# New durations in the cost tables of a list scheduler that orders one Trainium2 kernel's instructions

## The chip, the cores and the metric

The kernel runs on one core of a Trainium2 chip. The metric is the device time of one execution in microseconds; the time before is the median of three runs. PE is the matmul engine, PEld its weight loads, DVE the vector engine, ACT the scalar (activation) engine, POOL the GpSimd engine and SP the engine that issues the DMAs.

## What is computed

256 tokens of 1024 columns go through two stacks of layers, all in float32.

- First stack, four layers: an attention (kinds a, b, c, then a again), a residual and a layer norm, then a feed-forward part (gate, up, silu, down; 2816 hidden columns), a residual and a layer norm.
- Second stack, two layers. Each has one wide projection of the normed tokens, from which four branches are made: a gated convolution, a sparse attention whose keys are the 64 of highest index score per token (found by eight rounds of "take the eight largest, then strike them out"), a gated linear recurrence, and an attention over 256 memory tokens. The branches are lifted to 1024 columns, gated, summed and projected; then comes a feed-forward part as above, with root-mean-square norms in front.

```python
def swiglu(x, w_gate_up, w_down):
    gu = x @ w_gate_up
    gate, up = gu[..., :D_FF], gu[..., D_FF:]
    return (jax.nn.silu(gate) * up) @ w_down
```

## The kernel before, in words

The tokens are two tiles of 128 (`t` = 0 and 1). Every product with weights is done in float32r with both operands split in two parts: `xT` (or `s`) as high and low part of the transposed tokens, `wh` and `wl` as high and low part of the weights; three matmuls of 128x128 by 512 columns per pair of 128 rows (`dense`, L377, its matmul is L390; the down product of the feed-forward part is L1113 to L1115). Weights come in pieces of 256 rows by 512 columns, in one fixed order (`loader`, L349): SP loads a piece into one of 4 `raw` buffers, ACT casts it to `wh` (L366), DVE subtracts to get `wl` (L371), and both tiles use it. There are 8 pairs of `wh`, `wl` buffers.

The smaller matmuls are plain float32: transposes of 128x128 blocks (L440), scores of two heads at a time (L628) and their products with the values (L649), the index scores (L1522), the memory attention (L1738, L1756) and the recurrence (L1949, L1987, L2006 and L2008). For a pair of heads the chain is: scores on PE (L628), mask and row minimum on DVE (L635), exponential with its sum on ACT (L642), reciprocal on DVE (L660), scaling on ACT or DVE (L665 or L668), transpose on PE (L440), copy on ACT or DVE (L451 or L454), product with the values on PE (L649).

**The order of the instructions is a planner's.** All tensors are handled by Python generators, each a chain of work. The class `Flow` (L114) runs them against a clock of its own while the program is written out, and the order in which they issue instructions is the order in every engine's queue. On the chip each engine works through its queue in that order, and semaphores alone hold an instruction back until its inputs are there. So the planner's durations set no time on the chip; they set the order. Each issue is booked:

- `op` (L218) adds a duration to the engine's planned busy time and returns its end plus `LAT`, the time at which the chain goes on.
- `act` (L223), `dve` (L230) and `pool` (L233) turn a number of elements per partition into a duration; `pe` (L236) moves the clock itself on and returns it plus `PELAT`.
- PE is given to the chain of lowest rank among those whose inputs are there by the planner's clock (`rank`, L173): transposes and attention matmuls have ranks 0 to 3, products with weights 5. ACT and DVE are given to the weight casts and subtractions and to some steps of the norms by `grant` (L182); all other steps on them are queued when their chain is resumed.
- `turned` (L447) and `shares` (L651) compare the planned busy times of ACT and DVE to choose which of the two does a copy or a scaling.
- `root` (L1313) is the inverse root of a norm, one POOL instruction (L1315); `rms_heads` (L1343) uses it between a sum and two multiplications on DVE.

```python
def op(self, eng, ns):
    end = max(self.busy[eng], self.cur) + ns
    self.busy[eng] = end
    return end + self.LAT
```

Of the kernel before, what the change touches and what calls it, by code (L numbers as in the profile page):

```python
# [17 lines left out]
S = 256  # L18
D = 1024
NT = S // P  # L20
# [14 lines left out]
SB = 217  # L35
PV = 135
# [33 lines left out]
class Buf:  # L70
    """A buffer out of a Slots, given back with free(when its last reader is through)."""
# [42 lines left out]
class Flow:  # L114
    """Puts the instructions of many chains of work into one order. A chain is a generator. It
    yields a time to go on at, an Event to wait for, a buffer to be given, or ("pe", rank) to
    be given the tensor engine, lowest rank first."""

    LAT = 250.0
# [53 lines left out]
    def rank(self, ask):  # L173
        """The first tile leads in the products with weights, but not by too much."""
        r = ask[0]
        if r == (5, 0) and self.lag > self.limit:
            r = (6, 0)
        elif r[0] == 5 and r[1] >= NT and self.soon:
            r = (4, r[1])
        return r, ask[1]  # L180

    def grant(self, eng):  # L182
        """Lets one of those go on that wait for the engine to be idle: the lowest rank first, and
        those of a rank above 0 not in an urgent stretch, unless they have waited long."""
# [3 lines left out]
        # weights come first when few are at hand  # L188
# [34 lines left out]
    def act(self, n, table=None):  # L223
        ns = n / 1.2 + 120
        if table is not None and table != self.table:
            self.table = table
            ns += 1300
        return self.op("act", ns)

    def dve(self, n):  # L230
        return self.op("dve", n / 0.96 + 75)

    def pool(self, n):  # L233
        return self.op("pool", n * 2.1 + 120)

    def pe(self, ns):  # L236
        # the clock is halved when the last 3.4 us were idle, until as many were busy
# [15 lines left out]
class Parts:  # L253
    """The two parts of a transposed operand, and when each stretch of them is there."""
# [25 lines left out]
class Net:  # L280
    def __init__(self, nc, tc, ctx, t_in, out):
# [22 lines left out]
        # the last token tile never finds all banks taken  # L304
        self.lead = Slots(f, MM - 1, lambda: None)
        # attentions of the second block at a time
# [5 lines left out]
    def pieces(self, tag, n):  # L312
        """Two ways to cut one buffer: for n pairs of heads of up to 768 keys, or 3 n pairs of up to
        256, each head with room for a sink."""
# [26 lines left out]
    def group(self, key, w, *ranges, rows=256):  # L341
        """The pieces of w [k, .], two k tiles each, for column ranges side by side."""
# [6 lines left out]
    def loader(self):  # L349
        nc = self.nc  # L350
        for piece in self.plan:
            shape = [P, piece.srcs[0].shape[1], sum(s.shape[2] for s in piece.srcs)]
            raw = yield self.raw.want(shape)
            at = 0
# [3 lines left out]
            self.f.spawn(self.split(piece, raw, shape, self.f.op("dma", shape[1] * shape[2] * 1.45) + 1800))  # L358
# [18 lines left out]
    def dense(self, t, xt, key, ps):  # L377
        """ps = x^T.T @ the group's pieces, three products per pair of operands, those that need a
        second part when it is there."""
# [5 lines left out]
        count = 0  # L385

        def product(a, b, j, k):
# [3 lines left out]
            f.pe(max(n, 384) / 2.4 + 2.5)  # L391
# [29 lines left out]
    def phase(self, t, name):  # L421
        """How many pieces of weights the first tile may be ahead."""
# [11 lines left out]
    def turn(self, blocks, rank):  # L434
        """The [128, 128] blocks transposed, side by side in a PSUM bank."""
# [8 lines left out]
    def turned(self, blocks, dst, rank):  # L444
        """dst [128, n, 128] = the blocks transposed."""
# [13 lines left out]
    def parts(self, h, l, blocks, rank, hev=None, lev=None):  # L459
        """h, l [128, n, 128] = the two parts of the blocks transposed."""  # L460
# [19 lines left out]
    def pair(self, n):  # L480
        """Room for the parts, with n events."""
# [4 lines left out]
    def parts_x(self, x, rank, hurried=False, late=0.0, then=None):  # L486
        """The two parts of the transpose of x [128, 1024]; the second half of x is there at the
        time late."""
# [33 lines left out]
    def setup(self):  # L522
        """What the first layer needs besides weights."""
# [13 lines left out]
        # angles, for [positions, token tile, frequency]  # L537
# [8 lines left out]
        # whole turns, split into a multiple of 4096 and a rest, are taken off in three steps  # L546
# [14 lines left out]
        # both into [-pi, pi]  # L561
# [10 lines left out]
        # per positions and token tile [128, 2, 2, 8]: cos | cos, and -sin | sin  # L572
# [12 lines left out]
    def rotate(self, q, nh, tab):  # L585
        """The first 16 of each of nh heads of q [128, nh, 64], in place; the time it is done."""
# [15 lines left out]
    def heads(self, t, two, l, m, left):  # L602
        """Two heads of one token tile, whose q^T and k^T lie in different halves of the rows. Each:
        its q^T per group; per PSUM bank a list of (group, k^T blocks [64, 128]) and the mask over
        them; the V blocks [128 keys, 64] in the same order; where its output's transpose goes,
        [64, 128]; what its -maximum starts from; minus its sink, if any. Their sums l and -maxima
        m; the count of pairs left and the event for the last."""
# [12 lines left out]
        for j in range(len(two[0][1])):  # L620
# [8 lines left out]
            yield f.pe(2 * SB * len(both[0][0]))  # L629
            for z, (head, (ks, mask), ps, s) in enumerate(zip(two, both, pss, scs)):  # L630
# [6 lines left out]
                ends[z] = f.dve(wb + 40)  # L637
                ps.free(ends[z])
            at += wb
        for z, s in enumerate(scs):  # L640
            yield ends[z]
            nc.scalar.activation(s[:, :w], s[:, :w], AF.Exp, scale=-1.0, bias=m[:, z:z + 1], accum_out=l[:, z:z + 1])  # L642
            end = f.act(n + 220, "exp")
# [7 lines left out]
        f.pe(2 * PV * nb)  # L651
# [1424 lines left out]
```

## Time and profile before

| | us |
|---|---|
| median of three runs | 2458.12 |
| lowest and highest of the three | 2455.24 and 2460.45 |
| span of the profiled execution, first to last instruction | 2453.7 |
| PE busy in it | 2416.1 (98%) |
| DVE, ACT, POOL busy in it | 1601.5 (65%), 1209.8 (49%), 116.0 (5%) |

The profiled execution's own time is not listed apart from its span; the runs lie 1.5 to 6.8 us above the span. A busy time is the union of an engine's instructions. Matmuls are pipelined and their ends are modelled, so the time that one matmul adds to a row of them is read from their starts, not from its duration. The granted clock (PEclk) is 1.00 when TensorE runs at the upper of its two levels (2.4 GHz) throughout a stretch, and 0.50 at the lower one.

### The profile page before, as it was taken

The page shows a single profiled execution, that of the slowest core. Times are in us where ns is not written, and L with a number is a line of the kernel's source. Part 1 is how long each engine was busy: PE and PEld are TensorE (multiplying, and loading weights), DVE is VectorE, ACT ScalarE, POOL GpSimd, SP SyncE. Part 2 cuts the span into 40 slices and gives each one's busy share as a digit, 9 for nine tenths or more (in the row PEclk, how much of TensorE's full clock was granted, in tenths as well). Part 3 has the DMA queues.
Part 4 walks back from the last instruction along what each step waited for, and adds up shares of the span by engine and source line. Part 5 has one row for each costly group of instructions (what it writes and reads, how often), then busy time and mean ns, then how long its engine had stood idle before and what let it go on. Part 6 is the DMA issues. An engine that isn't in the chain of part 4 may idle for free.

```text
span 2453.7 us, 32501 instructions
## 1 busy us (share of the span) xinstructions
PE 2416.1 (98%) x12163; PEld 1953.6 (80%) x12163; DVE 1601.5 (65%) x2600; ACT 1209.8 (49%) x1779; POOL 116.0 (5%) x151
## 2 busy tenths in 40 slices
PE   8999999999999999999999999999999999999999
PEld 6688888888888778887788778878888778878887
DVE  7754666567546675467854887676754786776544
ACT  5544445455444654446544456444544465445443
POOL 0000000000000000010000100111000100111000
PEclk9999999999999999999999999999999999999999
DMA  7365563544656446554665536655765445655654
GB/s 240 114 208 170 175 220 115 162 129 155 196 167 195 152 149 206 168 184 134 206 199 172 180 112 182 179 155 178 235 187 168 142 139 160 181 152 190 192 172 129
DMA packets 226238, 419.84 MB, mean 171 GB/s; under 512 B 18048, under 2 KB 66848, under 8 KB 226080
## 3 DMA queue, kind: packets, MB, share of 16 engines
q1 hardware_dynamic: 226080, 417.76, 55.2%
q8 instruction: 95, 1.56, 0.3%
q14 instruction: 63, 0.52, 0.1%
HBM read 416.66 MB, written 1.05 MB: 170 GB/s over the span
## 4 chain that ended last, share of the span: by engine, by line
PE 94%; DVE 3%; ACT 1%; DMA 1%; issue 0%; POOL 0%; SPq 0%; DVEq 0%; ACTq 0%; POOLq 0%
PE mm L390 68%; PE acc L440 5%; PE acc L1113 5%; PE acc L1115 5%; PE acc L1114 5%; PE acc L628 2%; PE acc L649 2%; DVE wl L371 1%; ACT wh L366 0%; DVE s L1537 0%; DVE s L1557 0%; DMA raw<-w_in 0%; PE acc L1738 0%; PE acc L1756 0%; PE acc L2008 0%
## 5 line engine op out<-in xcount | busy, mean ns | idle before, releaser
L390 PE MATMUL mm<-wh,xT 128*128 128x512 f32 x5056 | 1642.5, 396 | 11.1 <-ACT wh L366 3.6
L371 DVE TENSOR_TENSOR wl<-raw,wh 128x1024 fp32r<-128x1024 f32 (+1 forms) x764 | 933.9, 1231 | 584.0 <-ACT wh L366 582.0
L366 ACT CAST wh<-raw 128x1024 fp32r<-128x1024 f32 (+1 forms) x764 | 795.8, 1046 | 804.8 <-PE mm L390 570.7
L390 PEld LDWEIGHTS mm<-wh,xT 128*128 128x128 f32 x5056 | 945.5, 188 | 218.1 <-issue 5.9
L390 PE MATMUL mm<-wl,xT 128*128 128x512 f32 x2528 | 973.2, 390 | 3.3 <-DVE wl L371 3.1
L390 PEld LDWEIGHTS mm<-wl,xT 128*128 128x128 f32 x2528 | 475.8, 189 | 95.7 <-DVE wl L371 5.2
L1113 PE MATMUL acc<-wh,s 128*128 128x512 f32 x528 | 211.7, 401 | 0.0
L1115 PE MATMUL acc<-wh,s 128*128 128x512 f32 x528 | 208.2, 394 | 0.0
L1114 PE MATMUL acc<-wl,s 128*128 128x512 f32 x528 | 208.1, 394 | 0.0
L1115 PEld LDWEIGHTS acc<-wh,s 128*128 128x128 f32 x528 | 99.2, 188 | 23.4
L1114 PEld LDWEIGHTS acc<-wl,s 128*128 128x128 f32 x528 | 99.4, 188 | 21.3
L1113 PEld LDWEIGHTS acc<-wh,s 128*128 128x128 f32 x528 | 99.3, 188 | 20.9
L440 PE MATMUL acc<-ident,s 128*128 128x128 f32 x624 | 94.7, 273 | 4.5 <-DVE s L1358 4.5
L440 PEld LDWEIGHTS acc<-ident,s 128*128 128x128 f32 x624 | 77.0, 140 | 26.0 <-DVE s L1358 5.2
L1315 POOL TENSOR_TENSOR brs<-brs,mhalf 128x1 f32<-128x1 f32 x28 | 24.9, 890 | 1464.4 <-DVE brs L942 1216.8
L464 ACT CAST xT<-acc 128x512 fp32r<-128x512 f32 x68 | 39.8, 586 | 93.0 <-PE acc L440 92.9
L642 ACT ACTIVATE sc<-sc,m 128x129 f32<-128x129 f32 (+5 forms) x128 | 67.1, 526 | 23.7 <-DVE m L635 23.6
L464 ACT CAST s<-acc 128x512 fp32r<-128x512 f32 (+1 forms) x72 | 39.6, 550 | 65.9 <-PE acc L440 65.7
L454 DVE COPY pT<-acc 128x512 f32<-128x512 f32 (+1 forms) x84 | 48.7, 597 | 35.2 <-PE acc L440 34.8
L469 DVE TENSOR_TENSOR xT<-acc,xT 128x512 fp32r<-128x512 f32 x68 | 46.7, 687 | 34.9 <-ACT xT L464 34.7
L1071 ACT ACTIVATE s<-mm 128x512 f32<-128x512 f32 (+1 forms) x72 | 40.3, 560 | 53.1 <-PE mm L390 52.7
L440 PE MATMUL acc<-ident,sc 128*128 128x128 f32 x368 | 58.3, 283 | 6.3 <-ACT sc L665 6.1
(187 smaller groups left out, 1447.8 us busy)
## 6 DMA issues: line engine op xcount, KB each, us to landing
raw<-w_gate_up SPq DMA_DIRECT2D x160, 512.0 KB, 4.0
raw<-w_in SPq DMA_DIRECT2D x144, 512.0 KB, 4.2
raw<-w_down SPq DMA_DIRECT2D x88, 512.0 KB, 3.3
raw<-ffn_w_up SPq DMA_DIRECT2D x80, 512.0 KB, 3.7
raw<-b_w_qkv SPq DMA_DIRECT2D x96, 256.0 KB, 3.1
raw<-ffn_w_down SPq DMA_DIRECT2D x44, 512.0 KB, 3.3
raw<-w_lift SPq DMA_DIRECT2D x32, 512.0 KB, 4.0
raw<-a_w_qkv SPq DMA_DIRECT2D x24, 512.0 KB, 5.2
```

The costliest lines, as they stand in the source:

```text
L366: nc.scalar.copy(h[:], raw[:])
L371: nc.vector.tensor_sub(l[:], raw[:], h[:])
L390: nc.tensor.matmul(ps, a[:, k, :], b[:, k % 2, :], start=count == 1, stop=count == 3 * (last + 1))
L440: nc.tensor.transpose(ps[:, j * P:(j + 1) * P], b, self.ident[:])
L454: self.nc.vector.tensor_copy(dst, p3)
L464: self.nc.scalar.copy(h, p3)
L628: nc.tensor.matmul(ps[:, b * P:(b + 1) * P], head[0][g], k, start=True, stop=True)
L642: nc.scalar.activation(s[:, :w], s[:, :w], AF.Exp, scale=-1.0, bias=m[:, z:z + 1], accum_out=l[:, z:z + 1])
L649: nc.tensor.matmul(head[3], head[2][b], pT[:, (z * nb + b) * P:(z * nb + b + 1) * P], start=b == 0, stop=b == nb - 1)
L1113: nc.tensor.matmul(a, hh[:, k, :], wh[:, 0, cs], start=ch == 0 and k == 0, stop=False)
L1114: nc.tensor.matmul(a, hh[:, k, :], wl[:, 0, cs], start=False, stop=False)
L1115: nc.tensor.matmul(a, hl[:, k, :], wh[:, 0, cs], start=False, stop=ch == 5 and k == nk - 1)
```

## The change

Only what the planner books is changed; every instruction's form stays as it is. The constants and formulas of `act`, `dve`, `pool`, `pe`, `loader`, `root` and `LAT` get other values, `act` and `dve` get a further argument for accumulator reads and per-partition scalars, and every group of small float32 matmuls is booked at `FP` = 112 ns a matmul plus `SWITCH` = 190 ns instead of `SB` = 217 ns a matmul. Comments and docstrings become empty lines, and two lines are added at the top, so line numbers after are higher by 2.

```diff
-SB = 217
-PV = 135
+FP = 112.0
+SWITCH = 190.0
+POINTER = 170.0
+SUM = 190.0
...
-    LAT = 250.0
+    LAT = 60.0
...
-    def act(self, n, table=None):
-        ns = n / 1.2 + 120
+    def act(self, n, table=None, more=0.0):
+        ns = 0.904 * n + 127 + more
...
-    def dve(self, n):
-        return self.op("dve", n / 0.96 + 75)
+    def dve(self, n, more=0.0):
+        return self.op("dve", n / 0.96 + 152 + more)
...
-        return self.op("pool", n * 2.1 + 120)
+        return self.op("pool", n * 2.3 + 130)
...
-            self.f.spawn(self.split(piece, raw, shape, self.f.op("dma", shape[1] * shape[2] * 1.45) + 1800))
+            self.f.spawn(self.split(piece, raw, shape, self.f.op("dma", shape[1] * shape[2] * 1.53) + 2000))
...
-            f.pe(max(n, 384) / 2.4 + 2.5)
+            f.pe(max(n / 2.4 * 1.0625, FP))
...
-            yield f.pe(2 * SB * len(both[0][0]))
+            yield f.pe(2 * FP * len(both[0][0]) + SWITCH)
...
-                ends[z] = f.dve(wb + 40)
+                ends[z] = f.dve(wb, 142.0)
...
-            end = f.act(n + 220, "exp")
+            end = f.act(n, "exp", POINTER + SUM)
...
-        f.pe(2 * PV * nb)
+        f.pe(2.2 * FP * nb + SWITCH)
...
-                ends.append(f.act(n))
+                ends.append(f.act(n, None, POINTER))
...
-                    end = f.pe(648)
+                    end = f.pe(690)
...
-        return self.f.pool(60 + n)
+        return self.f.op("pool", 1050.0)
...
-            end = f.pe(2 * SB * (t + 1))
+            end = f.pe(2 * FP * (t + 1) + SWITCH)
...
-        yield f.pe(2 * SB * NT)
+        yield f.pe(4 * FP * NT + SWITCH)
...
-        end = f.pe(4 * SB)
+        end = f.pe(8 * FP + SWITCH)
...
-        end = f.pe(1950)
+        end = f.pe(16 * FP + SWITCH)
```

## Rows read from the trace of the kernel before

**Rows 1.** The page: the span, and each engine's busy time, share and instructions.

```profile
span 2453.7 us, 32501 instructions
...
PE 2416.1 (98%) x12163; PEld 1953.6 (80%) x12163; DVE 1601.5 (65%) x2600; ACT 1209.8 (49%) x1779; POOL 116.0 (5%) x151
```

**Rows 2.** Busy time by stretch: length, busy per engine, granted clock, DMA share, GB/s.

```profile
0.00:45.00 45.00, 37.30 (x173) 30.30 (x174) 31.87 (x74) 21.97 (x25) 2.73 (x22) 1.00 0.73 245
45.00:85.00 40.00, 33.21 (x227) 21.78 (x226) 33.92 (x115) 27.88 (x82) 3.19 (x16) 0.91 0.50 161
85.00:1120.00 1035.00, 1030.14 (x5308) 835.69 (x5307) 644.08 (x1015) 505.48 (x707) 17.08 (x24) 1.00 0.55 170
1120.00:1175.00 55.00, 51.30 (x346) 36.46 (x346) 43.37 (x125) 38.04 (x113) 4.39 (x21) 0.94 0.30 96
...
1380.00:1455.00 75.00, 71.34 (x402) 55.63 (x402) 66.82 (x194) 41.48 (x88) 10.29 (x8) 1.00 0.46 141
...
1900.00:1975.00 75.00, 68.13 (x359) 54.71 (x358) 59.54 (x153) 34.63 (x64) 6.90 (x6) 0.98 0.46 135
1975.00:2454.00 479.00, 474.94 (x2290) 386.81 (x2288) 302.58 (x411) 228.70 (x314) 32.38 (x23) 1.00 0.55 166
```

**Rows 3.** The chain that ended last: start, length, what.

```profile
2055.38 61.94 PE mm L390 x273
```

**Rows 4.** Timeline, 1960 to 1971 us: start, length, engine, line [idle before, releaser].

```profile
1964.91 0.28 DVE L1535 MAX8 m<-s 128x8 f32<-128x128 f32 x1
...
1965.50 0.42 DVE L1535 MAX8 m<-s 128x8 f32<-128x256 f32 x1
...
1966.36 0.28 DVE L1535 MAX8 m<-s 128x8 f32<-128x128 f32 x1
...
1969.53 0.50 PE L390 MATMUL mm<-wl,xT 128*128 128x512 f32 x1 [2.56 <-DVE wl L371]
```

**Rows 5.** Timeline, 1908 to 1923 us.

```profile
1915.77 1.10 ACT L464 CAST xT<-acc 128x512 fp32r<-128x512 f32 x2
...
1917.00 1.92 POOL L1315 TENSOR_TENSOR ss<-ss,mhalf 128x4 f32<-128x4 f32 x1 [2.92 <-DVE ss L1352]
...
1918.96 0.69 DVE L1355 TENSOR_TENSOR s<-mm,ss 128x512 f32<-128x512 f32 x1 [0.31 <-POOL ss L1315]
...
1920.43 0.80 PE L440 MATMUL acc<-ident,s 128*128 128x128 f32 x4 [4.19 <-DVE s L1358]
```

**Rows 6.** Groups by line and shape: count | busy us, mean ns | idle before.

```profile
L366 ACT CAST wh<-raw 128x1024 fp32r<-128x1024 f32 x756 | 791.7, 1052 | 791.1 <-PE mm L390 560.9 <-PE acc L1115 128.2 <-DMA raw<-w_in 14.3
...
L371 DVE TENSOR_TENSOR wl<-raw,wh 128x1024 fp32r<-128x1024 f32 x756 | 929.4, 1238 | 578.8 <-ACT wh L366 576.9
...
L1315 POOL TENSOR_TENSOR ss<-ss,mhalf 128x4 f32<-128x4 f32 x12 | 14.6, 1221 | 63.7 <-DVE ss L1352 63.7
```

**Rows 7.** Timeline, 45 to 85 us (first attention).

```profile
51.28 0.62 PE L440 MATMUL acc<-ident,sc 128*128 128x128 f32 x2 [1.78 <-ACT sc L665]
...
53.66 2.92 ACT L366 CAST wh<-raw 128x1024 fp32r<-128x1024 f32 x3
...
55.12 3.48 DVE L371 TENSOR_TENSOR wl<-raw,wh 128x1024 fp32r<-128x1024 f32 x3
...
66.16 0.50 ACT L642 ACTIVATE sc<-sc,m 128x257 f32<-128x257 f32 x1
...
66.66 0.50 ACT L642 ACTIVATE sc<-sc,m 128x257 f32<-128x257 f32 x1
```

**Rows 8.** Timeline, 1126 to 1140 us (last attention of kind a).

```profile
1130.01 0.40 PE L390 MATMUL mm<-wl,xT 128*128 128x512 f32 x1
...
1130.34 0.49 PE L628 MATMUL acc<-s,s 64*128 64x128 f32 x4
...
1130.76 0.50 PE L390 MATMUL mm<-wh,xT 128*128 128x512 f32 x1
...
1131.10 0.40 PE L390 MATMUL mm<-wl,xT 128*128 128x512 f32 x1
```

More of the change, by code (lines that the diff above doesn't have):

```diff
@@ L929, in square @@
         self.nc.scalar.activation(out, src, AF.Square, scale=1.0 / 32, bias=bias, accum_out=acc)
-        return self.f.act(out.shape[-1] + 220)
+        return self.f.act(out.shape[-1], None, POINTER + SUM)
     def norm(self, t, r, old, gb, st):
@@ L1747, in recall_two @@
                                  accum_out=l[:, z:z + 1])
-            end = f.act(S + 220, "exp")
+            end = f.act(S, "exp", POINTER + SUM)
         ps.free(end)
@@ L1757, in recall_two @@
                                  pT[:, (NT * z + b) * P:(NT * z + b + 1) * P], start=b == 0, stop=b == NT - 1)
-        pT.free(f.pe(2 * SB * NT))
+        pT.free(f.pe(4 * FP * NT + SWITCH))
         self.through(left)
@@ L1987, in hgrn @@
                 nc.tensor.matmul(ps[:, h * P:(h + 1) * P], ken[rr, h, :], v[rr, h, :], start=True, stop=True)
-            yield f.pe(4 * SB)
+            yield f.pe(8 * FP + SWITCH)
             s2 = yield self.s.want([P, 4, P])
```

## The prediction

> **What bounds the kernel now.** I read the page first: PE is busy for 2416.1 of 2453.7 us [rows 1], so 37.6 us of idle PE is all that an order alone can win, apart from how fast PE's own work runs. The second view is the busy time by stretch [rows 2]; the reader is to subtract PE's busy time from each length. The start loses 7.70 us (0 to 45) and the last stretch 4.06 us; the one waits for first loads, the other holds the way out, and I count neither. What is left lies in five stretches: 6.79 us (45 to 85, first attention), 4.86 (85 to 1120), 3.70 (1120 to 1175, the other attention of kind a), 3.66 (1380 to 1455, first layer of the second stack) and 6.87 (1900 to 1975, its second layer), 25.9 us in all. In three of them the granted clock is 0.91, 0.94 and 0.98: stretches at the lower of the two levels (1.2 GHz, against 2.4) that follow idle PE. At 0.09 x 40, 0.06 x 55 and 0.02 x 75 they cost at most 8.4 us more. So at most some 34 us, 1.4%, can be won. The third view, the chain that ended last, gives PE's pace: 273 products in 61.94 us, 0.2269 us each [rows 3]. The planner booked 215.8 ns, 5% too fast, and books 226.7 after.
>
> The last views are timelines of the waits, to see whether a wait comes from a wrong booking, which the change can mend, or from a lack of other work, which it can't.
>
> **The change part by part.** The same instructions are issued (the counts of matmuls, casts and DMAs stay), so nothing is added or removed on any engine. Every term is a wait that moves, and the sum is made against the span of 2453.7 us; the median of the runs, 2458.1, is 4.4 us longer, and I carry the difference over.
>
> *The eight rounds of the index selection.* A round is two DVE operations of n columns each. On the chip a round of 128 columns goes from 1964.91 to 1965.50 (0.59 us) and one of 256 from 1965.50 to 1966.36 (0.86) [rows 4]. Before, they were booked at 2 x (n / 0.96 + 75), that is 0.42 and 0.68 us; after, at 2 x (n / 0.96 + 152), 0.57 and 0.84. Both tiles' rounds run in turn, so eight of each were booked 8 x (0.17 + 0.18) = 2.8 us short. Behind them in DVE's queue stands a subtraction that makes wl, and PE waits 2.56 us for it at 1969.53 [rows 4]. The new booking is short by 8 x 0.04 = 0.3 us only, so that subtraction goes ahead of some of the rounds, or other products ahead of its own. I take 2.3 us as won; cover for the rounds pushed back is there, since the sparse branch is the third to be lifted.
>
> *The same code in the first layer of the second stack*: PE idle 3.66 us while DVE is busy for 66.8 of 75 [rows 2]. I take half, 1.8 us; the bounds are 0 and 3.66.
>
> *The root of a norm.* POOL takes 1221 ns on average for four heads [rows 6], and 1.92 us at 1917.00, where PE then waits 4.19 us for transposes that hang on it [rows 5]. From the root's start to the transposes pass 3.43 us; the old booking was 254 + 250 for the root and 2 x 608 + 250 for the two multiplications, 1.97 us; the new one is 1110 + 2 x 685 + 60, 2.54 us. The casts of another operand end at 1916.87 [rows 5], so products with weights could run, but they stand behind the transposes. Transposes booked 0.57 us later let two or three products of 0.227 past: 0.6 us won. The low clock after this wait stays, as most of the wait does.
>
> *LAT from 250 to 60, and longer operations.* POOL ends at 1918.92 and DVE starts at 1918.96 [rows 5]: a hand-off is 0.04 us, so 60 covers it. A DVE operation of 512 columns on the path was booked at 608 + 250 = 858 ns and takes 0.69 + 0.04; it is now booked at 745. Plans were late by 0.13 us a step and are now late by 0.01: still on the safe side, so I see no new waits from it. In the attentions the steps of a pair hardly change: exponential plus sum of 256 columns 767 before, 778 after; scaling 583 and 588. So the 10.5 us idle there (6.79 and 3.70) are mostly no error of booking: PE waits for ACT, 1.78 us at 51.28 [rows 7], when the projections are through and little else is there. Bounds 0 and 10.5; I take 2 us, nearer to none, for the copies that come 0.11 to 0.15 us earlier.
>
> *85 to 1120 us*: 4.86 us in 1035; I take 0, with the same to either side as bounds.
>
> *Weights, DMAs, POOL's and SP's queues.* A piece is booked at 1053 + 1219 ns for ACT and DVE (973 + 1142 before; rows say 1052 and 1238 [rows 6]); against 12 products of 0.227, 2.7 us, either fits. DMAs are booked 0.28 us later a piece; SP's queue holds them in the same fixed order of pieces, and a load waits for a free buffer, not for the booking: 0. POOL is busy for 5% [rows 1]: 0. Copies and scalings that change from ACT to DVE or back by the planned busy times cost PE nothing where both are under 65%: 0.
>
> Sum: 2.3 + 1.8 + 0.6 + 2.0 = 6.7 us, from 2453.7 to 2447.0 of span, or 2458.1 to **2451** us.
>
> **The rivals.** *Slower: pairs are booked too far apart.* The durations of a row are not what an engine needs per instruction when it runs several. Three casts in a row take 2.92 us with the last at 1.05, so 0.94 apart, and three subtractions 3.48, so 1.12 apart [rows 7]; booked are now 1.05 and 1.22. Exponentials of 257 columns start 0.50 us apart (66.16, 66.66) [rows 7]; booked were 0.52, and are now 0.72. With the scalings a pair of heads of 256 keys now takes 2 x 718 + 2 x 528 = 2.5 us of ACT's plan instead of 1.7. So its later pairs become ready in the plan one by one, and where two groups of small matmuls stood side by side, products with weights come between. The Trainium skill (Perfetto Trace Analysis, Optimizing Scalar/DVE Operations) says that a profiled duration holds a write acknowledgement which overlaps the next instruction; the rows agree (1.238 us long, 1.12 apart), and by that rule the change books both engines too full.
>
> What an extra alternation costs: from the product at 1130.01 over two small matmuls (four records) to the second product after them, 1131.10, pass 1.09 us; less two products at 0.227 this is 0.64 [rows 8]. Of it 0.10 is the way in (0.33 instead of 0.227) and 0.11 the way out, and the matmuls themselves stay. So an alternation costs between 0.21 and 0.64 us; I take the middle, 0.43. The code has 214 groups of small matmuls other than transposes (112 of scores, 88 with values, 14 of the recurrence). If one in eight loses its neighbour, 27 x 0.43 = 11.6 us, and the waits that I count as won come back elsewhere: 2458.1 + 11.6 = **2470** us. It decides from some 16 more alternations (6.7 / 0.43) on. For it speaks that the plan's shift is large on ACT; against it, that a mask and a copy on DVE lie between the pairs anyway, and that shorter hand-offs work the other way.
>
> *No change.* The waits come from a lack of other work: both tiles go through the same steps close behind one another, and when one wait is mended the next dependency shows. The change then does not do what it says where it matters: the order around a wait stays as it is. The 1.78 us at 51.28, and the 4.19 of which the new booking covers 0.57, speak for it. **2458** us.
>
> *Faster by more.* Better bookings let products with weights fill half of the 25.9 us and of the 8.4 at the low clock: 17 us, **2441** us. For it speaks that products with inputs ready did stand behind a wait (1916.87 against 1920.43); against it, that only the rounds and the root were booked far off.
>
> **How the numbers follow.** About 0.2% (5 us) is what a measurement of this kernel can tell from no change: its three runs lie 5.2 us apart. Any new order of 32501 instructions shuffles waits by some us, so I leave the chances wide: the forecast 0.36 (its own range 2446 to 2455), more 0.14, no change 0.22, slower 0.28. Faster by over 0.2% (under 2453.2) holds the case of more and nearly all of the forecast's, 0.48; within 0.2% the case of no change and the forecast's rest, 0.24; slower 0.28. The range reaches from the larger gain, 2441, to the price of the slower rival, 2470; beyond lie one in ten on either side.
>
> **What would show it.** Right: at the end of the selection in both layers of the second stack PE waits for wl under 0.5 us; the stretch 1900 to 1975 has 3 us less idle PE; products with weights stand between the root of the memory keys and their transposes; matmul counts are the same. The slower rival: PE's busy time rises above 2416 us by several us, with idle time the same or less, and more changes between L628 or L649 and L390. No change: the five stretches keep their idle time, or trade it. Wrong altogether would be a new wait of several us for wh or wl after an attention, or a low clock in more places.

## The result: slower by 0.76%, and the profile after

| | before | after |
|---|---|---|
| median of four runs, us | 2457.46 (2455.24 to 2460.45) | 2474.26 (2471.89 to 2477.24) |
| ratio, 95% interval | | 1.0076 (1.0063 to 1.0090) |
| span of the profiled execution | 2453.7 | 2472.9 |
| PE idle in it | 37.6 | 48.6 |

The changed kernel is 17 us slower by the medians, 19 by the ratio; 2451 us was foretold, with 2470 as the upper end. In the code after, every line number is higher by 2. The page of the kernel after, span and engines:

```profile
span 2472.9 us, 32489 instructions
...
PE 2424.3 (98%) x12163; PEld 1959.2 (79%) x12163; DVE 1596.8 (65%) x2596; ACT 1212.7 (49%) x1783; POOL 117.3 (5%) x151
```

Against [rows 1], PE has the same 12163 matmuls, 8.2 us more busy time and 11.0 us more idle time; that is the 19.2 us of span. The products themselves did not get slower, as one row of the chain that ended last shows (start, length, what): 16.34 us for 72, 0.2269 us each, as in [rows 3].

```profile
171.26 16.34 PE mm L392 x72
```

So the busy time grew elsewhere. Busy time by stretch of the kernel after, columns as in [rows 2]:

```profile
45.00:90.00 45.00, 36.72 (x242) 26.02 (x241) 32.74 (x114) 28.09 (x91) 6.44 (x16) 0.85 0.37 119
90.00:570.00 480.00, 479.05 (x2616) 390.78 (x2614) 300.61 (x489) 235.22 (x319) 5.41 (x4) 1.00 0.51 164
570.00:625.00 55.00, 51.10 (x281) 41.74 (x281) 40.11 (x62) 28.15 (x37) 2.05 (x2) 0.97 0.48 158
...
1130.00:1190.00 60.00, 54.75 (x354) 39.58 (x353) 45.73 (x119) 38.22 (x104) 3.17 (x16) 0.91 0.30 97
...
1390.00:1485.00 95.00, 90.41 (x506) 71.68 (x506) 81.92 (x224) 52.61 (x117) 10.64 (x10) 0.98 0.42 133
1485.00:1915.00 430.00, 429.06 (x2043) 350.29 (x2042) 278.19 (x344) 208.26 (x258) 29.99 (x24) 1.00 0.57 184
1915.00:1990.00 75.00, 67.90 (x332) 54.47 (x331) 53.20 (x128) 34.25 (x59) 7.46 (x7) 0.95 0.49 150
```

And one stretch of the kernel before, which [rows 2] holds only as part of a longer one:

```profile
560.00:615.00 55.00, 53.87 (x334) 44.17 (x335) 43.66 (x69) 30.94 (x41) 1.47 (x2) 1.00 0.55 171
```

Idle is length less busy; the price of the clock is at most (1 - granted clock) x length, since PE is idle in some of that time anyway. The stretches after start up to 15 us later and are up to 20 us longer, to hold the same work; both columns in us:

| stretch | idle before, after | clock before, after |
|---|---|---|
| first attention | 6.79, 8.28 | 3.6, 6.8 |
| end of the attention of kind b | 1.13, 3.90 | 0, 1.7 |
| last attention of kind a | 3.70, 5.25 | 3.3, 5.4 |
| first layer of the second stack | 3.66, 4.59 | 0, 1.9 |
| second layer of the second stack | 6.87, 7.10 | 1.5, 3.8 |
| sum | 22.2, 29.1 | 8.4, 19.5 |

These five short stretches hold 7 of the 11.0 us more idle and up to 11 us more of the lower clock, most of the loss; between them (90 to 570, 1485 to 1915) PE is busy for 99.8% of the time at full clock. I also counted the products of dense groups along both traces and compared the start of the same count: after is late by 3.7 us at 110, 2.8 at 520, 7.4 at 604, 12.5 at 1192, 13.9 at 1497, 15.5 at 1890 and 20.1 at 1940 us (times of before). The loss comes in steps, at those places, and stays nearly flat between them.

Part of the first step is a wait for loads. The setup of the second stack transposes two small constants in the first attention; in the kernel after, PE reaches them 4 to 5 us after their loads were issued and waits 2.04 us; before, it came to them 7.6 us after and did not wait. The rest of that stretch's idle time is 6.24 us, no more than the 6.79 before. After:

```profile
63.59 0.20 PE L1265 MATMUL acc<-ident,lbrows 8*128 8x8 f32 x1 [1.03 <-DMA lbrows<-hgrn_lower_bounds]
...
64.79 0.45 PE L1267 MATMUL acc<-ident,cwr 12*128 12x12 f32 x2 [1.01 <-DMA cwr<-conv_w]
```

Before:

```profile
70.75 0.22 PE L1263 MATMUL acc<-ident,lbrows 8*128 8x8 f32 x1
```

**A wait that the prediction did not see.** The stretch at the end of the attention of kind b has the cleanest step, 4.6 us: 2.7 us come with one wait and the lower clock behind it, most of the rest with two waits of 0.85 and 0.73 us (606.88 and 608.70) in the feed-forward part that follows. The first wait is the one to explain. The timeline of the kernel after (start, length, engine, line [idle before, releaser]):

```profile
573.72 0.92 ACT L644 ACTIVATE sc<-sc,m 128x768 f32<-128x768 f32 x1
574.54 0.18 ACT L644 ACTIVATION_READ_ACCUMULATOR sc<-sc,m 128x1 f32 x1
574.61 1.22 DVE L373 TENSOR_TENSOR wl<-raw,wh 128x1024 fp32r<-128x1024 f32 x1
574.64 0.92 ACT L644 ACTIVATE sc<-sc,m 128x768 f32<-128x768 f32 x1
...
577.00 0.39 PE L392 MATMUL mm<-wh,xT 128*128 128x512 f32 x1
577.43 0.69 DVE L985 SCALAR_TENSOR_TENSOR x<-x,mm 128x512 f32<-128x512 f32 x1 [1.60 <-PE mm L392]
...
578.76 0.15 DVE L662 RECIPROCAL l<-l 128x2 f32<-128x2 f32 x1
578.95 1.97 ACT L667 ACTIVATE sc<-sc,l 128x768 f32<-128x768 f32 x2 [2.38 <-DVE l L662]
...
579.71 4.43 PE L442 MATMUL acc<-ident,sc 128*128 128x128 f32 x24 [2.32 <-DVE bmv L942]
...
606.88 0.66 PE L442 MATMUL acc<-ident,s 128*128 128x128 f32 x4 [0.85 <-DVE s L1085]
...
608.70 0.50 PE L392 MATMUL mm<-wh,xT 128*128 128x512 f32 x1 [0.73 <-ACT xT L466]
```

The second row closes the exponentials of the first pair of heads at 574.72, so its reciprocal (L662) could have run at 575.83, after the subtraction. But in DVE's queue it stands behind the residual of the other tile (L985), and DVE sits idle for 1.60 us until the last product with weights has ended (577.39). So the reciprocal starts 2.9 us late, the scaling (L667) with it, and PE, which has just done its last product, waits until it can transpose the scaled scores. The row says bmv, a DVE operation at 579.48; what the transposes read is the scaling. The same place before:

```profile
572.71 0.16 DVE L660 RECIPROCAL l<-l 128x2 f32<-128x2 f32 x1
...
574.23 0.93 ACT L665 ACTIVATE sc<-sc,l 128x768 f32<-128x768 f32 x1
574.52 1.57 PE L440 MATMUL acc<-ident,sc 128*128 128x128 f32 x12
574.72 0.69 DVE L983 SCALAR_TENSOR_TENSOR x<-x,mm 128x512 f32<-128x512 f32 x1
...
576.05 0.15 DVE L660 RECIPROCAL l<-l 128x2 f32<-128x2 f32 x1
...
577.22 1.71 PE L440 MATMUL acc<-ident,sc 128*128 128x128 f32 x12 [1.13 <-ACT sc L665]
```

There the first pair's reciprocal stands ahead of the residual (L983), and its twelve transposes follow the products without a gap; only the second pair's transposes wait, 1.13 us.

The bookings allow the swap. The exponentials stand 0.92 us apart on the chip. Before, each was booked (768 + 220) / 1.2 + 120 = 943 ns, near that. After, it is 0.904 x 768 + 127 + 360 = 1181 ns, even more than the 1.00 us from the start of one to the end of its read (573.72 to 574.72), and the read overlaps the next exponential. So the two exponentials of a pair are booked 0.48 us longer than before, the four 0.95; the hand-off behind them is booked 0.19 us shorter, so a pair's reciprocal is planned some 0.29 us later. A residual can then be ready first in the plan, while on the chip the exponentials are early and the residual is late. That this alone made the swap is argued, not shown; the runs below that change one part bear on it.

### The profile page after: what moved, and what is told of

It is laid out like the page before. It is cut to its first block, busy times and chain, and to the rows that moved or that the text cites. A ratio compares the mean times of both kernels' runs of the same rounds, so it can differ in the third digit from the quotient of the medians.

```text
span 2472.9 us, 32489 instructions
## 1 busy us (share of the span) xinstructions
PE 2424.3 (98%) x12163; PEld 1959.2 (79%) x12163; DVE 1596.8 (65%) x2596; ACT 1212.7 (49%) x1783; POOL 117.3 (5%) x151
## 4 chain that ended last, share of the span: by engine, by line
PE 94%; DVE 3%; ACT 1%; DMA 1%; issue 1%; POOL 0%; SPq 0%; DVEq 0%; ACTq 0%; POOLq 0%
PE mm L392 68%; PE acc L442 5%; PE acc L1115 5%; PE acc L1117 5%; PE acc L1116 5%; PE acc L651 2%; PE acc L630 2%; DVE wl L373 1%; ACT wh L368 0%; DMA raw<-w_in 0%; PE acc L1524 0%; PE acc L2010 0%; PE acc L1989 0%; PE acc L1758 0%; DMA raw<-a_w_qkv 0%
## 5 line engine op out<-in xcount | busy, mean ns | idle before, releaser
L442 PEld LDWEIGHTS acc<-ident,s 128*128 128x128 f32 x624 | 76.4, 141 | 29.1 <-DVE s L1360 5.0
L456 DVE COPY pT<-acc 128x512 f32<-128x512 f32 (+1 forms) x77 | 45.1, 597 | 38.5 <-PE acc L442 38.0
L1073 ACT ACTIVATE s<-mm 128x512 f32<-128x512 f32 (+1 forms) x72 | 40.3, 560 | 50.0 <-PE mm L392 49.5
```

Of the source, the lines that this page charges most:

```text
L442: nc.tensor.transpose(ps[:, j * P:(j + 1) * P], b, self.ident[:])
```

## The experiments

Theories at the start. **A**: a duration is not what an engine needs per instruction; ACT and DVE are booked too full. **B**: 60 ns of hand-off leaves a plan without slack. **C**: any new order costs, since the old one is a chosen one; later in a sharper form, the planner's other settings fit the old bookings. **D**: groups of small matmuls are booked too short. **E**: with products booked at their true pace, the plan puts too few under each step. F and G, below, are rivals of the sharper C. No experiment changes which operations are done, only their order and which of ACT and DVE does a copy or a scaling. In two of the orders, e5_dense and e8_occ, the kernel's result is off by 4.9% all the same, so some step there depends on the order by more than the plan says; which one is not known. Both are timed with the same matmuls as the others, but carry less weight. The table has all medians, the ratio to before with its interval, and PE's idle time in the profiled execution (its span less PE busy). Where the text says what a run costs, it is the ratio less one, times 2456 us:

| run | median us | ratio (95%) | PE idle us |
|---|---|---|---|
| e1_lat | 2458.64 | 1.0017 (1.0007 to 1.0026) | 38.2 |
| e2_pe | 2476.53 | 1.0090 (1.0073 to 1.0106) | 50.1 |
| e3_dur | 2481.86 | 1.0112 (1.0096 to 1.0128) | 49.5 |
| e4_lat245 | 2455.76 | 1.0001 (0.9991 to 1.0011) | 38.7 |
| e5_dense | 2462.03 | 1.0025 (1.0013 to 1.0037) | 40.5 |
| e6_small | 2465.70 | 1.0037 (1.0026 to 1.0048) | 40.5 |
| e7_lat_occ | 2469.27 | 1.0057 (1.0040 to 1.0074) | 41.3 |
| e8_occ | 2471.99 | 1.0060 (1.0035 to 1.0085) | 46.7 |
| e9_dense_mid | 2464.89 | 1.0040 (1.0028 to 1.0052) | 38.5 |
| e10_lat300 | 2460.92 | 1.0016 (1.0005 to 1.0028) | 39.9 |
| e11_pelat260 | 2458.50 | 1.0012 (1.0001 to 1.0023) | 38.9 |
| e12_after_bc5 | 2475.33 | 1.0078 (1.0048 to 1.0107) | 50.5 |
| e13_tuned | 2467.80 | 1.0043 (1.0030 to 1.0057) | 43.4 |
| e14_pitch | 2470.44 | 1.0060 (1.0043 to 1.0078) | 44.0 |
| e15_pitch_tuned | 2455.39 | 1.0000 (0.9991 to 1.0009) | 43.0 |
| e16_cross | 2463.14 | 1.0030 (1.0018 to 1.0041) | 40.7 |
| e17_equal1 | 2464.34 | 1.0043 (1.0028 to 1.0058) | 49.3 |
| e18_equal2 | 2458.67 | 1.0021 (1.0010 to 1.0031) | 38.3 |

### The change in three parts, each alone in the kernel before

e1_lat, the hand-off alone:

```diff
-    LAT = 250.0
+    LAT = 60.0
```

> The kernel before with LAT at 60 instead of 250 and nothing else of the change. Theory A (engines overbooked: the durations of ACT and DVE are latencies, and plan a pair's steps too far apart) expects no loss from this part: 2453 to 2461 us. Theory B (a hand-off without slack: a chain is resumed so early that PE's queue holds instructions whose inputs are just not there) expects most of the loss here: 2469 to 2477 us, with PE idle for 45 us or more. Theory C (the order before is a lucky one among many near-equal orders, and any shuffling costs about the same) expects 2463 to 2475 us here and in every other part alone.

e2_pe, all bookings of PE (the lines with `SB`, `PV`, 648 and 1950, and `dense`):

```diff
-            f.pe(max(n, 384) / 2.4 + 2.5)
+            f.pe(max(n / 2.4 * 1.0625, FP))
...
-            yield f.pe(2 * SB * len(both[0][0]))
+            yield f.pe(2 * FP * len(both[0][0]) + SWITCH)
```

> The kernel before with only PE's bookings of the change (products at 226.7 ns, groups of small matmuls at 112 ns a matmul plus 190). Theory A and theory B expect no loss: 2453 to 2461 us, or a small gain, since the booking of a product now agrees with its pace in the trace. Theory C expects 2463 to 2475 us.

e3_dur, the bookings of ACT, DVE, POOL, DMA and the root, with LAT still 250:

```diff
-        ns = n / 1.2 + 120
+        ns = 0.904 * n + 127 + more
...
-        return self.op("dve", n / 0.96 + 75)
+        return self.op("dve", n / 0.96 + 152 + more)
```

> The kernel before with only the bookings of ACT, DVE, POOL and the DMAs of the change, LAT at 250. Theory A expects the whole loss here or more, 2470 to 2482 us, since chains are booked even later than in the change, with LAT on top. Theory B expects none, 2453 to 2461 us. Theory C expects 2463 to 2475 us.

The hand-off costs 4 us, PE's bookings 22, the durations 28: B falls as the main cause. The parts do not add up: together they cost 19 us, less than either of the two large ones.

### Controls: does any other order cost?

e4_lat245 and e10_lat300 change LAT by little, e11_pelat260 the end of PE's work:

```diff
-    LAT = 250.0
+    LAT = 245.0
```

> A control: the kernel before with LAT at 245 instead of 250, a change of 2% in one booking that means nothing by itself, but gives another order. Theories A and B expect the time of before, 2453 to 2461 us. Theory C expects an order about as bad as any other: 2463 to 2475 us, or in any case a move of 5 us or more.

```diff
-    LAT = 250.0
+    LAT = 300.0
```

> A control without any claim to truth: the kernel before with LAT at 300 instead of 250, all else as before. Hand-offs are booked still later than they are, so no theory of a truer or a tighter plan says anything of it. Theory C expects a loss of 4 to 20 us, 2460 to 2476 us, at the same places as in the other runs; if it takes the time of before, 2452 to 2459 us, then the losses so far belong to the bookings that were changed and not to any new order.

```diff
-PELAT = 200.0
+PELAT = 260.0
```

> A second control of the kind: the kernel before with PELAT at 260 instead of 200, so that results of PE are booked 60 ns later. Theory C expects 2460 to 2476 us; if the losses belong to the changed bookings, 2452 to 2459 us.

They cost 0, 4 and 3 us. A reshuffle as such costs little, so C in its first form gives a fifth of the loss at most; but none of the three is faster than before.

### PE's bookings in halves

```diff
-            f.pe(max(n, 384) / 2.4 + 2.5)
+            f.pe(max(n / 2.4 * 1.0625, FP))
...
-                    end = f.pe(648)
+                    end = f.pe(690)
```

> The kernel before with one part of PE's bookings alone: products with weights at 226.7 ns (and 690 for three down products), their pace in the trace, instead of 215.8 (648). The second run lost 22 us with all of PE's bookings. Theory D (the groups of small matmuls are now booked too short, so the plan crowds the attention steps) expects no loss here: 2450 to 2460 us. Theory E (with the products' true pace the plan has 5% fewer of them under every step of ACT and DVE, whose bookings stay as they were) expects most of the 22 us here: 2468 to 2478 us. Theory C (any shuffling of this size costs) expects 2463 us or more here and in the next run too.

e6_small takes the other lines of e2_pe: `FP` and `SWITCH` in place of `SB`, `PV` and 1950.

```diff
-            yield f.pe(2 * SB * len(both[0][0]))
+            yield f.pe(2 * FP * len(both[0][0]) + SWITCH)
...
-        f.pe(2 * PV * nb)
+        f.pe(2.2 * FP * nb + SWITCH)
```

> The kernel before with the other part of PE's bookings alone: groups of small matmuls at 112 ns a matmul plus 190 a group instead of 217 a matmul. Theory D expects most of the 22 us here, 2468 to 2478 us; theory E expects none, 2450 to 2460 us; theory C 2463 us or more.

```diff
-            f.pe(max(n, 384) / 2.4 + 2.5)
+            f.pe(max(n, 384) / 2.4 + 8.0)
...
-                    end = f.pe(648)
+                    end = f.pe(664)
```

> The kernel before with products booked at 221.3 ns (and 664 for three down products), half-way to the true pace; the whole way cost 6 us. Theory E (the loss grows with the pace booked) expects about half of it, 2457 to 2461 us. Theory C (each new order draws its own waits at the few places where both tiles run out of products) expects no relation: it may be worse than the whole way or as good as before, anywhere from 2453 to 2475 us.

Products cost 6 us, small groups 9, both together 22. Half of the correction of the products costs 10, not half of 6 (the two intervals overlap): no grading, so E falls as a law, and D explains its 9 us only.

Most of these 9 us are lost at the end of the attention of kind b, and by another order than in the changed kernel: by the count of products e6_small is 2.4 us late at 545 and 9.2 at 604. The first pair's reciprocal stands ahead of the residual there (577.07 against 577.39 us), but the second pair's (581.77) stands behind two steps of the norm that start at 580.45, and PE waits 3.00 us. In e2_pe the same wait is 3.37 us:

```profile
584.92 1.97 PE L440 MATMUL acc<-ident,sc 128*128 128x128 f32 x8 [3.37 <-ACT sc L665]
```

### Occupancy instead of duration

e7_lat_occ is e1_lat and e3_dur together, e8_occ the changed kernel, both with this:

```diff
-        self.busy[eng] = end
+        self.busy[eng] = end - {"act": 100.0, "dve": 80.0}.get(eng, 0.0)
```

> The kernel before with LAT at 60 and the new bookings of ACT, DVE, POOL and the DMAs, but an engine is held for 100 ns (ACT) or 80 ns (DVE) less than an instruction's booked duration, as the starts in a row show (three casts 0.94 us apart, three subtractions 1.12); the chain still goes on at the booked end. PE's bookings as before. Theory A (overbooked engines) expects this to lose nothing, 2450 to 2460 us, since the third run lost 27 us with the bookings too full. Theory C expects 2463 us or more.

> The changed kernel with the same correction: ACT and DVE held for 100 and 80 ns less than the booked duration. All of the planner's numbers then agree with the trace to a few per cent. If the change was slow because its numbers were still wrong (theory A, with the loss of PE's part a loss of being out of step with the others), this gives 2450 to 2460 us. Theory C, in which a truer plan is no better than another, expects 2463 to 2480 us.

Both stay at 1.006: A is not the whole cause. How much the correction won in e7_lat_occ is not known, since the two parts without it were not run together. e7_lat_occ also tells what the swap needs. It has it, with PE's bookings as before, while in e1_lat and in e3_dur the first pair's reciprocal stands ahead of the residual (570.26 against 572.92 us, 584.86 against 586.56). So neither the hand-off nor the durations alone gave the swap, and PE's bookings were not needed for it:

```profile
576.58 0.69 DVE L985 SCALAR_TENSOR_TENSOR x<-x,mm 128x512 f32<-128x512 f32 x1 [1.38 <-PE mm L392]
...
577.91 0.15 DVE L662 RECIPROCAL l<-l 128x2 f32<-128x2 f32 x1
```

In e8_occ the step at the end of the attention of kind b is gone by the count of products (1.2 us late at 520, 0.9 at 604), though the reciprocal still stands behind the residual there; PE's wait is 1.18 us instead of 2.32, because more products were left. The correction was also too small: an exponential of 768 columns still holds ACT for 1.08 us in the plan, and stands 0.92 apart.

### One setting of the planner

```diff
-LAGS = {"a": 4, "bc": 3, "out": 5, "ffn": 2, "end": 6, "in": 5, "out2": 3}
+LAGS = {"a": 4, "bc": 5, "out": 5, "ffn": 2, "end": 6, "in": 5, "out2": 3}
```

> The changed kernel with one tuning value moved: in the attention layers of kinds b and c the first tile may be 5 pieces of weights ahead instead of 3. If the new loss at the end of the b layer (4.6 us between the first 1800 and 2050 products) comes from the two tiles' meeting there, one in its norm and one at the end of its attention, a larger lead changes it by 3 us or more, most likely for the better: 2466 to 2472 us. If the loss is in the bookings themselves, whatever the lead, the time stays at 2472 to 2477 us with the same loss at that place.

It gains nothing at the end: by the count of products it is 6.7 us ahead of the changed kernel at 520 us, 4.3 at 604, 0.8 at 1192 and level at the last. One lead moved alone moves the steps to other places.

### Settings chosen for the new bookings

The planner's own clock stops at some time when the plan is made. That is a number of the source and no time of the chip, but settings can be searched by it. e13_tuned does so for the changed kernel:

```diff
-SLACK = 150.0
+SLACK = 600.0
...
-LAGS = {"a": 4, "bc": 3, "out": 5, "ffn": 2, "end": 6, "in": 5, "out2": 3}
-ENDCH = 4
+LAGS = {'a': 5, 'bc': 3, 'out': 2, 'ffn': 1, 'end': 8, 'in': 5, 'out2': 3}
+ENDCH = 5
...
-AUTO = -200.0
+AUTO = 800.0
...
-SCA = 600.0
+SCA = 0.0
...
-STOCK = 4
+STOCK = 3
```

> The changed kernel with six of the planner's other settings chosen again (the leads LAGS, ENDCH, SLACK, AUTO, SCA, STOCK), so that the planner's own clock, with the new bookings, ends 29.5 us earlier than with the old settings (2452.8 us booked against 2482.3). Theory C (the settings were fitted to the old bookings, and the new bookings are unfitted to them): most of the 29.5 us shows, 2445 to 2458 us, idle PE under 42 us. Rival F (what the planner books as idle is not what the chip leaves idle, so its clock can't choose an order): 2465 to 2478, idle PE 44 us or more.

e14_pitch keeps the old settings and the old bookings of ACT and DVE (near the distance of two starts), takes PE's bookings of e2_pe, and:

```diff
-    LAT = 250.0
+    LAT = 130.0
```

> Before, with all PE bookings of the change, LAT 130, and ACT, DVE, POOL, DMA and root booked as before: before's ACT and DVE formulas lie near the distance between the starts of two operations in a row (exponential of 768 columns booked 0.94 us, starts 0.92 apart; mask step of 256 booked 0.38, starts 0.41 apart), so engines are not overbooked, and the hand-off covers the rest of a latency. Theory A (overbooked ACT and DVE make most of the loss): 2455 to 2462 us. Rival (the PE bookings cost their 20 us whatever ACT and DVE are booked at): 2470 to 2478. Theory C has no sharp number here, 2458 to 2475.

e15_pitch_tuned is e14_pitch with searched settings:

```diff
-SLACK = 150.0
+SLACK = 400.0
...
-LAGS = {"a": 4, "bc": 3, "out": 5, "ffn": 2, "end": 6, "in": 5, "out2": 3}
+LAGS = {'a': 9, 'bc': 2, 'out': 8, 'ffn': 1, 'end': 9, 'in': 3, 'out2': 8}
...
-AUTO = -200.0
+AUTO = 200.0
...
-SCA = 600.0
+SCA = 0.0
...
-PATIENCE = 3000.0
+PATIENCE = 500.0
...
-STOCK = 4
+STOCK = 3
```

> The same bookings as the run with LAT 130 and PE bookings, with the planner's settings chosen again for its own clock (2406.1 us booked against 2424.3). Theory C with A: the best of all, 2438 to 2452 us, idle PE under 35 us. F: within 5 us of the run with the same bookings and old settings.

e16_cross is before, with the settings of e13_tuned (the diff above, in before's source).

> Control: before, old bookings, with the settings chosen for the new bookings (the planner's own clock ends at 2337.7 us against 2338.5). Theory C: the settings help only with the bookings they were chosen for, so 2462 to 2475 us. Rival (the settings are simply better): 2440 to 2452. F: no relation, 2456 to 2475.

With the changed bookings, new settings win back 8 us (1.0076 to 1.0043) of the 29.5 that the planner's clock promised: C's 2445 to 2458 is missed, F's 2465 holds (its idle time of 44 us or more does not quite: 43.4). With engines booked at their pace they win back 15 us of 18 (1.0060 to 1.0000), which F does not allow, though C's 2438 to 2452 is missed by 3 us too, and its idle time under 35 us by 8. With the old bookings the settings of e13_tuned cost 7 us, which both C and F had allowed. At the end of the attention of kind b, the timeline of e13_tuned has the first pair's reciprocal ahead of the residual again, and PE's wait falls to 1.01 us:

```profile
575.03 0.16 DVE L662 RECIPROCAL l<-l 128x2 f32<-128x2 f32 x1
575.23 0.94 ACT L667 ACTIVATE sc<-sc,l 128x768 f32<-128x768 f32 x1 [0.59 <-DVE l L662]
...
576.98 1.47 PE L442 MATMUL acc<-ident,sc 128*128 128x128 f32 x12
577.18 0.69 DVE L985 SCALAR_TENSOR_TENSOR x<-x,mm 128x512 f32<-128x512 f32 x1 [1.33 <-PE mm L392]
...
579.46 1.50 PE L442 MATMUL acc<-ident,sc 128*128 128x128 f32 x12 [1.01 <-DVE bmv L942]
```

By the count of products it goes from 3.2 us late at 520 to 2.6 at 604, where the changed kernel goes from 2.8 to 7.4: the step comes and goes with the length of that wait and the low clock behind it. e14_pitch, which books exponentials at 943 ns, has no idle PE there at all and loses most of its 15 us later, in the second stack. Its busy time in that stretch:

```profile
560.00:615.00 55.00, 55.00 (x347) 45.03 (x347) 44.56 (x75) 29.58 (x40) 2.33 (x2) 1.00 0.52 168
```

And e15_pitch_tuned in three of the five stretches:

```profile
45.00:90.00 45.00, 39.57 (x278) 28.20 (x277) 33.68 (x124) 30.34 (x92) 4.44 (x21) 0.96 0.36 123
...
1120.00:1180.00 60.00, 56.20 (x370) 41.16 (x369) 46.90 (x122) 40.54 (x94) 1.89 (x6) 1.00 0.39 120
...
1895.00:1985.00 90.00, 81.50 (x422) 64.91 (x421) 68.26 (x178) 46.43 (x88) 8.34 (x8) 0.96 0.47 145
```

PE is idle for 43.0 us in the whole of it, 5.4 more than before, and the span is the same: the clock is 0.96 and 1.00 in the two attentions of kind a, where it was 0.91 and 0.94 [rows 2], and PE's busy time is 6.1 us less (2410.0 against 2416.1).

### Was e15 a lucky draw?

Two further sets of settings for the bookings of e15_pitch_tuned, found by a longer search:

```diff
-LAGS = {'a': 9, 'bc': 2, 'out': 8, 'ffn': 1, 'end': 9, 'in': 3, 'out2': 8}
+LAGS = {'a': 8, 'bc': 2, 'out': 6, 'ffn': 1, 'end': 7, 'in': 5, 'out2': 3}
...
-ORD = ("idx", "iq", "dq", "mq", "cx", "cc", "cb")
+ORD = ('iq', 'dq', 'mq', 'idx', 'cb', 'cc', 'cx')
...
-LOW = 0
+LOW = 1
...
-AUTO = 200.0
+AUTO = 800.0
...
-SCA = 0.0
+SCA = 300.0
```

> The bookings of the run e15 (LAT 130, PE bookings, ACT and DVE as before) with settings found by a longer search; the planner's own clock ends at 2403.8 us against 2406.1 there. C (settings and bookings have to fit, and the plan's clock ranks orders): 2449 to 2456 us, no slower than e15. G (e15 was a lucky draw among orders that book alike): anywhere from 2455 to 2472.

```diff
-SLACK = 400.0
+SLACK = 200.0
...
-LAGS = {'a': 9, 'bc': 2, 'out': 8, 'ffn': 1, 'end': 9, 'in': 3, 'out2': 8}
-ENDCH = 4
-HOT = "iq"
-ORD = ("idx", "iq", "dq", "mq", "cx", "cc", "cb")
+LAGS = {'a': 8, 'bc': 2, 'out': 2, 'ffn': 1, 'end': 8, 'in': 3, 'out2': 6}
+ENDCH = 5
+HOT = 'idx'
+ORD = ('dq', 'cx', 'idx', 'mq', 'iq', 'cb', 'cc')
...
-SCA = 0.0
+SCA = 300.0
...
-PATIENCE = 500.0
+PATIENCE = 3000.0
...
-STOCK = 3
+STOCK = 6
```

> The same with other settings, the planner's own clock at 2404.5 us. C: 2449 to 2457 us, within 4 us of e17. G: the two lie 5 us or more apart, or both above 2460, since bookings 2 us apart say nothing of the chip's order.

They cost 11 and 5 us where e15_pitch_tuned cost none: three orders that the planner holds equal (2403.8 to 2406.1 us by its clock) are spread over 11 us, as G says. e15_pitch_tuned and e18_equal2 are clearly better than e14_pitch (15), e17_equal1 only by its median, so the settings matter, but the plan's clock doesn't tell orders apart within that spread. In e17_equal1 new idle time has come up late, 12.0 us from 1985 us on, where before had 4.06 in its last stretch [rows 2]:

```profile
1985.00:2460.00 475.00, 462.96 (x2240) 373.49 (x2238) 300.60 (x452) 229.66 (x318) 28.61 (x21) 1.00 0.51 163
```

**What stands and what stays open.** Shown: the loss is waits at a few places where both tiles run out of products, with the lower clock after some of them. At one of them, 2.7 us, it is a reciprocal that stands behind a waiting residual, and the loss goes when it stands ahead again (e13_tuned) or when enough products are left (e8_occ). Supported: the order of before fits its own bookings and settings, and a changed booking asks for changed settings (8 to 15 us of the loss come back with them). No run beats before. Open: which part of the change sets which of the other steps, and why e2_pe and e3_dur cost 22 and 28 us where the change as a whole costs 19. The swap came where hand-off and durations were changed together; which of the durations it needs was not tried. e8_occ, which holds ACT 0.10 us less for each exponential, still has it.

## Why the prediction was wrong, point by point

**What bounds the kernel**: right. The 37.6 us of idle and the lower clock were where time could go either way, and the five stretches that it named hold most of the change; the end of the attention of kind b lies in the long one, 85 to 1120 us, which it set to 0.

**The eight rounds**: the mechanism was right, the term not. The 2.56 us wait of [rows 4] is gone, but waits for wl of 0.48 and 1.52 us came up at 1399.10 and 1401.35, ahead of the selection in the first layer; all waits of PE for wl are now 2.5 us over four places. Waits of PE after (engine, what it ran and what it waited for: us, times, longest), and before:

```profile
PE acc L442 <- ACT sc L667: 6.7, 7, 1.9
...
PE acc L442 <- DVE s L1360: 3.7, 2, 3.5
...
PE mm L392 <- DVE s L1357: 2.5, 2, 2.3
PE mm L392 <- DVE wl L373: 2.5, 4, 1.5
PE acc L442 <- DVE bmv L942: 2.3, 1, 2.3
```

```profile
PE acc L440 <- ACT sc L665: 6.1, 5, 2.2
PE acc L440 <- DVE s L1358: 4.5, 2, 4.2
...
PE mm L390 <- DVE wl L371: 3.1, 2, 2.6
...
PE mm L390 <- DVE s L1355: 1.7, 1, 1.7
```

The total for wl fell by 0.6 us, not by 2.3.

**The root**: right in size by luck. The wait of 4.19 us is 3.54 at 1936.24, 0.65 less where 0.6 was foretold. But no product runs between the root and its transposes, which still come 3.44 us after the root's start (3.43 before): the wait is shorter because the eight transposes ahead of it came later, after a new wait of 0.73 us of their own. And another wait came up in the same layer, 2.31 us for the multiplication L1357; the 1.7 us for that line before lay in the first layer. The clock fell to 0.95, and the layer holds 7.10 us of idle instead of the 3 us less that was to be seen.

```profile
1931.41 1.29 PE L442 MATMUL acc<-ident,x 128*128 128x128 f32 x8 [0.73 <-DVE x L1340]
...
1932.80 1.93 POOL L1317 TENSOR_TENSOR ss<-ss,mhalf 128x4 f32<-128x4 f32 x1 [2.96 <-DVE ss L1354]
1934.77 0.69 DVE L1357 TENSOR_TENSOR s<-mm,ss 128x512 f32<-128x512 f32 x1 [0.31 <-POOL ss L1317]
1936.24 1.11 PE L442 MATMUL acc<-ident,s 128*128 128x128 f32 x4 [3.54 <-DVE s L1360]
...
1952.68 0.47 PE L392 MATMUL mm<-wh,xT 128*128 128x512 f32 x1 [2.31 <-DVE s L1357]
```

**First layer of the second stack**: 1.8 us won was a guess of one half; idle rose by 0.9 us.

**DMAs**: set to 0, with the loads of weights alone in view. Two waits for other loads in the first attention made 2.04 us.

**LAT and longer operations: the step that failed.** "Still on the safe side, so I see no new waits from it" and "in the attentions the steps of a pair hardly change". Hand-off and duration were added up for one step of one chain of 256 columns, 767 against 778. What a plan orders by is also when an engine is free, and there nothing cancels: four exponentials of 768 columns are booked 0.95 us longer. Those of the layer of kind b, the widest, were not costed, and 85 to 1120 us was set to 0. It lost 2.7 us at the end of that attention, by a wait of 2.32 us (1.13 before) and the lower clock behind it, and 2 more in the feed-forward part. The two attentions of kind a, from which 2 us were to be won, lost 3 us by idle time (2 of them the waits for loads) and up to 5 by the clock.

**The slower rival**: its time, 2470, was near, and its premise holds for the exponentials of 768 columns too, booked 1.18 us for starts 0.92 apart. The Trainium skill (Perfetto Trace Analysis, Optimizing Scalar/DVE Operations) says that part of a profiled duration overlaps the next instruction; the rows here agree, 1.00 us to the end of the read against starts 0.92 apart. But the rival's price was wrong. Runs of products are broken off 355 times after, against 361 before, so there are no more alternations; PE's busy time rose with the time at the lower clock, and idle time rose too. What an overbooked engine costs was a wait behind the wrong instruction in a queue, not a switch.

**The last line of the prediction**, "a new wait of several us for wh or wl after an attention, or a low clock in more places", is near what came: a wait of 2.32 us at 579.71, though for scaled scores and not for wh or wl, and the lower level in seven places instead of four. It was named as a sign and given no price; the range ended 4 us too low.

## What to carry to other kernels

A list scheduler's numbers do no more than rank what is ready; truer numbers gave another order here, not a better one, and settings that were chosen with the old ones have to be chosen again. An engine's booking (the distance of two starts) and a chain's (the time to its result) are two numbers; booking them so, with settings chosen again, reached the time of before and no more. When costing such a change, add up the bookings of each engine over a row of instructions and ask which of two queues' heads will now be waiting for the bottleneck. Three orders that the plan held equal differed by 11 us here (0.4%), so a gain of 7 us foretold from the bookings alone is within the draw.

## What was not expected of the hardware

A wait of PE can be paid twice. The lower level (1.2 GHz) came after waits in seven places of the kernel after, four before, and PE's busy time rose by 8.2 us with the same matmuls. Not every wait has it behind it: after the 2.56 us of [rows 4] the clock stayed at 1.00. Two of the seven, as busy time by stretch (granted clock third from the end):

```profile
580.00:583.40 3.40, 3.40 (x19) 3.40 (x18) 3.40 (x6) 2.10 (x4) 0.64 (x1) 0.55 0.00 0
1935.00:1941.80 6.80, 5.56 (x18) 4.69 (x19) 3.02 (x5) 0.52 (x1) 0.00 (x0) 0.52 0.12 28
```

So idle time alone does not rank orders: e15_pitch_tuned has 43.0 us of idle PE and the span of before (2453.0), with a mean clock of 0.998 against 0.996; e13_tuned has 43.4 us and a span of 2461.7, with 0.994.
